# Gate and up of two feed-forward layers by Strassen's 2x2 block product

## Chip, cores and metric

The kernel runs on one core of one Trainium2 chip. The metric is the device time of one execution in microseconds (us), given as the median of several runs. The times of single instructions come from one execution that the hardware profiler recorded.

## What is computed

One inference step of a two-layer decoder trunk on 520 tokens (512 of a prompt, 8 of a sample group), with 1024 features, all in fp32. Each layer runs a SwiGLU feed-forward layer (`ffn1`), a mixer (layer 0: a chunked gated MLP; layer 1: the S5 state-space mixer), cross-attention into 256 memory tokens, and a second feed-forward layer (`ffn2`). The change touches the feed-forward layers of layer 1:

```python
def _swiglu(h, wg, wu, wd):
    return (jax.nn.silu(h @ wg) * (h @ wu)) @ wd
...
        x = x + 0.5 * _swiglu(_rmsnorm(x, norm_ffn1[i]), ffn1_wg[i], ffn1_wu[i], ffn1_wd[i])
```

`wg` and `wu` are 1024 x 2816, `wd` is 2816 x 1024. The keys and values of the memory tokens (`_mem_kv`) are also outputs.

## The kernel before

The activations stay in SBUF in transposed form, `X`: eight tiles of 128 features by 520 tokens. Products are made exact enough by splitting each fp32 operand into a high part, rounded to the fast fp32r type, and a low part that holds the rest; a product is then three matmuls (high x high, high x low, low x high). A matmul has 128 x 128 weights and 260 moving columns, half of the tokens, since an accumulation tile (`ps`, four of them in a ring) has two halves.

A weight block of 256 columns is loaded by SyncE's DMA queue into a raw buffer (`wr`, a ring of three). ScalarE copies the high part (`wh`), and VectorE, or GpSimd for every fourth call, subtracts to get the low part (`wl`); both are rings of four tiles (`wsplit`). So a weight can be split as soon as the one four before it has been used.

A feed-forward layer goes through eleven blocks of gate and up columns (`gu`). A block has 2 x 2 products of eight 128-row steps. VectorE scales each result by the norm's factor on its way out of PSUM, ScalarE applies SiLU, VectorE multiplies, and the hidden tile is split in two parts for the next product. After some blocks `down` multiplies the hidden tiles so far and accumulates into `X`; the gate-up blocks run one ahead of the groups in `FFN_GROUPS`.

Work of other stages is filled in between: each block and each `down` ends with `fill()`, which runs one step of a generator. `s5_prep` (25 steps, line 901) builds the tables of the S5 mixer, mostly with small VectorE and GpSimd instructions; it is spread over `ffn2` of layer 0 and `ffn1` of layer 1, followed by the first two steps of `mem_kv` for layer 1 (line 415: norm of the memory tokens, then their transposes). The other eight steps of `mem_kv`, the chunks of keys and values, are filled into the S5 mixer (line 1146). That mixer first needs the norm (sum of squares, `rs_tok`, `rs_diag`, `rs_row`), then runs a loop over eight feature tiles, each with a scan on VectorE.

The kernel is written as a program order; a scheduler sets the order in which the instructions of one engine stand, and each engine then runs its own list in order. Tiles that are asked for wait for the release of the tile that had the buffer. Temporaries (`t`, also `e1` to `e3` after the change) come from one ring.

## Time and profile before

| | |
|---|---|
| median of three runs | 2488.09 us (2486.79 to 2488.33) |
| the profiled execution | 2482.45 us, span 2480.7 us |
| TensorE busy | 2412.5 us (97%), 20159 matmuls |
| VectorE / ScalarE / GpSimd busy | 1343.5 (54%) / 799.7 (32%) / 558.2 us (23%) |

The profile's busy times of TensorE include the pipeline of overlapping matmuls: the 284 ns of one matmul is its own length, and the distance from one to the next is read by counting matmuls in a stretch. PE is TensorE, DVE is VectorE, ACT is ScalarE, POOL is GpSimd and SP is SyncE; PEld are the weight loads. A line such as L74 is a line of the kernel before; helpers collect many operations on one line, so the names of the tiles matter more.

### The profile page before, as it was taken

The numbers are of one execution on the slowest core, as the hardware profiler recorded it, in microseconds if no ns is written. First come the engines' busy times: TensorE is split into PE (matmuls) and PEld (weight loads), VectorE is DVE, ScalarE is ACT, GpSimd is POOL, SyncE is SP. The second block draws the span as 40 slices with busy tenths as digits, with TensorE's granted clock in tenths as the row PEclk, the third lists the DMA queues.
The fourth block names the chain that finished last, engine by engine and source line by source line (L and its number), as shares of the span: only waits on it lengthen the run. The fifth ranks groups of instructions, "written<-read, shape, count | busy, mean of one in ns | idle before, by whom it ended". The sixth has DMA issues, their size and how long they took to land.

```text
span 2480.7 us, 46682 instructions
## 1 busy us (share of the span) xinstructions
PE 2412.5 (97%) x20159; PEld 2341.0 (94%) x20159; DVE 1343.5 (54%) x2304; ACT 799.7 (32%) x1219; POOL 558.2 (23%) x532
## 2 busy tenths in 40 slices
PE   8999999999999999999999999999879999999998
PEld 7999999999999799999999999998669969999998
DVE  6534344648556557455556644546974655434344
ACT  4323222432224242232343423324322334222223
POOL 2111011102111012262522515203552101101111
PEclk9999999999999999999999999999989999999999
DMA  5243432421225623324233333325723562232321
GB/s 172 90 132 120 136 103 86 120 86 59 89 93 190 230 94 91 103 94 142 98 115 103 128 107 112 132 82 179 257 93 107 170 238 86 85 104 81 99 77 52
DMA packets 235147, 293.33 MB, mean 118 GB/s; under 512 B 6910, under 2 KB 203254, under 8 KB 234942
## 3 DMA queue, kind: packets, MB, share of 16 engines
q1 hardware_dynamic: 221831, 254.87, 31.9%
q10 hardware_dynamic: 12567, 34.38, 4.0%
q8 instruction: 159, 2.61, 0.4%
q0 software_dynamic: 544, 1.10, 0.3%
q14 instruction: 46, 0.38, 0.0%
HBM read 264.77 MB, written 25.56 MB: 117 GB/s over the span
## 4 chain that ended last, share of the span: by engine, by line
PE 87%; DVE 7%; issue 2%; ACT 1%; POOL 1%; DMA 1%; DVEq 0%; ACTq 0%; SPq 0%; POOLq 0%
PE ps L74 86%; PE ps L77 1%; DVE ld L1216 1%; DVE v L795 1%; DVE xs L280 1%; DVE wl L113 1%; DVE sq L224 1%; DVE t L555 0%; DVE hid L151 0%; POOL ld L1212 0%; ACT e L575 0%; DVE bi L1115 0%; DVE t L358 0%; POOL ld L1226 0%; DMA wr<-in_x_wv 0%
## 5 line engine op out<-in xcount | busy, mean ns | idle before, releaser
L74 PE MATMUL ps<-xs,wh 128*128 128x260 f32 x7168 | 1165.6, 284 | 3.4 <-ACT xs L279 2.4
L74 PEld LDWEIGHTS ps<-xs,wh 128*128 128x128 f32 x7168 | 990.9, 189 | 7.2 <-ACT xs L279 2.9
L110 ACT ACTIVATE wh<-wr 128x1024 fp32r<-128x1024 f32 (+2 forms) x408 | 386.5, 950 | 1079.2 <-PE ps L74 984.5
L74 PE MATMUL ps<-xs,wl 128*128 128x260 f32 x3584 | 726.2, 283 | 0.0
L113 POOL TENSOR_TENSOR wl<-wr,wh 128x1024 fp32r<-128x1024 f32 (+2 forms) x107 | 241.8, 2260 | 1507.9 <-ACT wh L110 1492.8
L74 PEld LDWEIGHTS ps<-xs,wl 128*128 128x128 f32 x3584 | 555.6, 189 | 0.0
L74 PE MATMUL ps<-hid,wh 128*128 128x260 f32 (+2 forms) x2816 | 456.7, 283 | 2.8 <-ACT hid L150 1.8
L74 PEld LDWEIGHTS ps<-hid,wh 128*128 128x128 f32 x2816 | 388.8, 188 | 4.8 <-ACT hid L150 2.2
L113 DVE TENSOR_TENSOR wl<-wr,wh 128x1024 fp32r<-128x1024 f32 (+2 forms) x301 | 341.7, 1136 | 86.2 <-ACT wh L110 85.2
L74 PE MATMUL ps<-hid,wl 128*128 128x260 f32 (+2 forms) x1408 | 288.2, 283 | 0.0
L74 PEld LDWEIGHTS ps<-hid,wl 128*128 128x128 f32 x1408 | 218.6, 188 | 0.0
L358 DVE TENSOR_TENSOR t<-ps,rs 128x520 f32<-128x520 f32 x88 | 61.4, 698 | 256.0 <-PE ps L74 256.0
L372 DVE SCALAR_TENSOR_TENSOR X<-ps,X 128x520 f32<-128x520 f32 x120 | 83.8, 698 | 210.3 <-PE ps L74 209.9
L356 DVE TENSOR_TENSOR t<-ps,rs 128x520 f32<-128x520 f32 x88 | 61.4, 698 | 183.7 <-PE ps L74 152.9
L151 DVE TENSOR_TENSOR hid<-t,hid 128x520 fp32r<-128x520 f32 x88 | 95.6, 1086 | 34.3 <-ACT hid L150 34.3
L150 ACT ACTIVATE hid<-t 128x520 fp32r<-128x520 f32 x88 | 56.3, 639 | 127.9 <-DVE t L359 127.8
L74 PE MATMUL ps<-o,wh 128*128 128x260 f32 x512 | 92.4, 290 | 1.2 <-DVE o L151 0.7
L74 PE MATMUL ps<-z,wh 128*128 128x260 f32 x512 | 84.2, 285 | 1.1 <-DVE z L151 0.5
L74 PE MATMUL ps<-um,wh 128*128 128x260 f32 x512 | 82.7, 284 | 0.0
L359 DVE TENSOR_TENSOR t<-t,t 128x520 f32<-128x520 f32 x88 | 78.9, 897 | 6.8 <-ACT wh L121 0.5
L74 PEld LDWEIGHTS ps<-o,wh 128*128 128x128 f32 x512 | 74.6, 188 | 7.4 <-issue 2.9
L74 PE MATMUL ps<-t,ld 128*32 128x136 f32 (+1 forms) x896 | 49.1, 326 | 26.2 <-POOL t L1221 9.2
(321 smaller groups left out, 2409.9 us busy)
## 6 DMA issues: line engine op xcount, KB each, us to landing
wr<-in_ffn_wg SPq DMA_DIRECT2D x43, 1024.0 KB
wr<-in_ffn_wu SPq DMA_DIRECT2D x43, 1024.0 KB, 5.5
wr<-in_ffn_wd SPq DMA_DIRECT2D x48, 768.0 KB, 4.2
wr<-in_a_w_in SPq DMA_DIRECT2D x16, 1024.0 KB, 6.1
kc<-in_cache_mem_k SPq DMA_DIRECT2D x32, 512.0 KB, 7.4
vc<-in_cache_mem_v SPq DMA_DIRECT2D x32, 512.0 KB, 6.1
wr<-in_x_wk SPq DMA_DIRECT2D x8, 1024.0 KB, 5.0
wr<-in_x_wv SPq DMA_DIRECT2D x8, 1024.0 KB, 5.7
```

The source lines that it names most:

```text
L74: self.nc.tensor.matmul(out, lhsT=lhsT, rhs=rhs, start=start, stop=stop)
L77: self.nc.tensor.transpose(out, in_, self.ident[base : base + k, base : base + k])
L110: nc.scalar.activation(hi, r, AF.Copy)
L113: eng.tensor_sub(lo, r, hi.bitcast(F32))
L150: nc.scalar.activation(sl[:, 0, n0:n1], src, AF.Copy)
L151: nc.vector.tensor_sub(sl[:, 1, n0:n1], src, sl.bitcast(F32)[:, 0, n0:n1])
L224: (nc.gpsimd if k == 7 and early or k < 4 and not early else nc.vector).tensor_add(sums[-1], sums[-1], t)
L280: self.nc.vector.scalar_tensor_tensor(s[:, 1, n0:n1], x, g, s.bitcast(F32)[:, 0, n0:n1], op0=ALU.mult, op1=ALU.subtract)
L356: nc.vector.tensor_mul(self.v2(t), pg[:, :, :HN], rs)
L358: nc.vector.tensor_mul(self.v2(w), pu[:, :, :HN], rs)
L359: nc.vector.tensor_mul(w, w, t)
L372: nc.vector.scalar_tensor_tensor(xv, p[:, :, :HN], 0.5, xv, op0=ALU.mult, op1=ALU.add)
```

## The change

In both feed-forward layers of layer 1 the first two gate-up blocks stay as they were (`PLAIN`); the other nine go through `gu7`. The 1024 input features and 256 columns of a block are cut in two, and the tokens are cut in two. With A the weights and B the inputs, seven products of half size replace eight. `seven_x` makes the combinations of the inputs once per layer, `seven` those of the weights in each block: S1 and S2 on GpSimd, S3 and the second S2 on VectorE. Results are collected in three accumulation tiles and three temporaries. All seven low parts of a block are VectorE's. The groups for `down` have four hidden tiles (two in the last). The raw buffers become four, the temporaries nine instead of twelve. `s5_prep` runs two steps per filling in `ffn2` of layer 0 alone, and all of `mem_kv` for layer 1 is filled into the S5 mixer, where two fillings follow each other behind `rs_diag` and the loop fills in all eight rounds.

```diff
+WR = 4
 FFN_GROUPS = ((0, 6), (6, 12), (12, 18), (18, 22))
-BUFS = {"t": 12, "rs": 2, "rt": 4, "st": 10, "sti": 4, "mv": 4, "sc": 2, "cj": 2, "s5": 12, "s5i": 1,
+SEVEN_GROUPS = ((0, 4), (4, 8), (8, 12), (12, 16), (16, 20), (20, 22))
+PLAIN = 2
+BUFS = {"t": 9, "rs": 2, "rt": 4, "st": 10, "sti": 4, "mv": 4, "sc": 2, "cj": 2, "s5": 12, "s5i": 1,
...
+    def seven_x(self, key, xs):
+        nc = self.nc
+        V = nc.vector
+        xb = [[self.slot([128, 4, HN], F32, "xb") for _ in range(2)] for _ in range(2)]
+        for k in range(KT):
+            for h in range(2):
+                nc.scalar.activation(xb[k // 4][h][:, k % 4], self.X[:, k, h * HN : (h + 1) * HN], AF.Copy,
+                                     scale=self.gcol(key, k))
+        (b11, b12), (b21, b22) = xb
+        V.tensor_sub(b11, b12, b11)
+        V.tensor_sub(b12, b22, b12)
+        V.tensor_sub(b22, b22, b11)
+        V.tensor_sub(b21, b21, b22)
+        T = []
+        for b in (b11, b22, b12):
+            hi, lo = (self.slot([128, 4, HN], F32R, "xt") for _ in range(2))
+            nc.scalar.activation(hi, b, AF.Copy)
+            V.tensor_sub(lo, b, hi.bitcast(F32))
+            T.append([(hi[:, k], lo[:, k]) for k in range(4)])
...
+        def last():
+            for k in range(4):
+                self.split(xs[k], b21[:, k], HN, NT)
+
+        return {"B11": B[0], "B21": B[2], "B22": B[3], "T1": T[0], "T2": T[1], "T3": T[2], "T4": B[1]}, last
+
+    def seven(self, r1, r2, ops, ps):
+        A11, A21, A12, A22 = r1[..., :128], r1[..., 128:], r2[..., :128], r2[..., 128:]
+        n, nk = sh[1:3]
...
+        def product(p, w, b, first):
+            hi, lo = w
+            for x in range(n):
+                for k in range(nk):
+                    bh, bl = ops[b][k]
+                    for i, (m, r) in enumerate(((hi, bh), (hi, bl), (lo, bh))):
+                        self.mm(p[:, x, :HN], m[:, x, k], r, first and k == 0 and i == 0, k == nk - 1 and i == 2,
+                                skip_group_check=not first)
+
+        S1, S2, S3 = (self.wp.tile(sh, F32, name=self.nm("S"), tag="S", bufs=3) for _ in range(3))
+        w11 = parts(A11)
+        G.tensor_add(S1, A21, A22)
+        G.tensor_sub(S2, S1, A11)
+        a, b, c = (ps() for _ in range(3))
+        va, vb, vc = (p[:, :, :HN] for p in (a, b, c))
+        e1, e2, e3 = (self.tmp([128, 2, HN]) for _ in range(3))
+        product(a, w11, "B11", True)
+        nc.scalar.copy(e1, va)
+        product(b, parts(S2), "T2", True)
+        V.tensor_add(e2, vb, e1)
+        product(a, parts(A12), "B21", False)
+        yield "11", va
+        V.tensor_sub(S3, A11, A21)
+        V.tensor_sub(S2, A12, S2)
+        product(b, parts(S3), "T3", False)
+        V.tensor_add(e3, vb, e1)
+        product(c, parts(S1), "T1", True)
+        V.tensor_add(e3, vc, e3)
+        yield "22", e3
+        product(b, parts(A22), "T4", False)
+        V.tensor_add(e1, vb, e1)
+        yield "21", e1
+        product(c, parts(S2), "B22", False)
+        V.tensor_add(e2, vc, e2)
+        yield "12", e2
...
+        def gu7(j):
+            if late:
+                late.pop()()
+            cs = slice(j * 256, (j + 1) * 256)
...
+            tw = [self.tmp() for _ in range(2)]
+            for name, v in self.seven(*r, ops, self.ps):
+                i, h = int(name[0]) - 1, int(name[1]) - 1
+                d = self.tmp([128, 2, HN]) if name == "11" else v
+                nc.vector.tensor_mul(d, v, rs[:, h : h + 1].to_broadcast([128, 2, HN]))
+                nc.scalar.activation(d[:, 0], d[:, 0], AF.Silu)
+                nc.vector.tensor_mul(tw[i][:, h * HN : (h + 1) * HN], d[:, 1], d[:, 0])
+                if name in ("21", "12"):
+                    hid[2 * j + i] = self.slot(name="hid")
+                    self.split(hid[2 * j + i], tw[i])
+            fill()
...
-                gu(done)
+                (gu7 if seven and done >= PLAIN else gu)(done)
                 done += 1
+                if seven and done == 1:
+                    ops, more = self.seven_x(key, xs)
+                    late.append(more)
...
-            nc.gpsimd.dma_start(bn[:, c], ins["b_b_" + n][0].rearrange("(q g) p c -> (g p) q c", g=2))
+            for q in range(0, NPAIR, 8):
+                nc.gpsimd.dma_start(bn[:, c, q : q + 8],
+                                    ins["b_b_" + n][0, 2 * q : 2 * q + 16].rearrange("(q g) p c -> (g p) q c", g=2))
...
         dg = self.rs_diag(sq)
         fill()
+        fill()
         rs = self.rs_row(dg)
...
-            if i < KT - 2:
-                fill()
+            fill()
...
-        self.ffn(0, False, steps(prep))
+        self.ffn(0, False, steps(prep, 2))
+        drain(prep)
         self.tap("ffn2_0")
-        pre = chain(prep, islice(gen := self.mem_kv(1, kv1), 2))
-        self.ffn(1, True, steps(pre))
-        drain(pre)
+        self.ffn(1, True, seven=True)
         self.tap("ffn1_1")
         self.pool_every = 2
+        gen = self.mem_kv(1, kv1)
         self.s5(steps(gen))
...
-        self.ffn(1, False, finish=self.final)
+        self.ffn(1, False, finish=self.final, seven=True)
```

VectorE, in `ffn1` of layer 1, where two gate-up blocks meet. Before (L356 and L358 scale gate and up, L113 is a low part, L151 the split of a hidden tile):

```order
L356 TENSOR_TENSOR t_15784<-ps_15686,rs_14258 128x520
L113 TENSOR_TENSOR wl_15949<-wr_15946,wh_15948 128x1024
L358 TENSOR_TENSOR t_15785<-ps_15687,rs_14258 128x520
L359 TENSOR_TENSOR t_15785<-t_15785,t_15784 128x520
L113 TENSOR_TENSOR wl_15953<-wr_15946,wh_15952 128x1024
L151 TENSOR_TENSOR hid_15790<-t_15785,hid_15790 128x520
```

And after, in the first block of a pair (L342 is a low part, L365, L371 and L373 the adds e2, e3, e3, L474 a scaling, L476 the gated product, L368 the S3 and L369 the second S2 of the next block):

```order
L342 TENSOR_TENSOR wl_15825<-S_15692,wh_15824 128x1024
L365 TENSOR_TENSOR t_15705<-ps_15702,t_15704 128x520
L342 TENSOR_TENSOR wl_15857<-wr_15687,wh_15856 128x1024
L474 TENSOR_TENSOR t_15789<-ps_15701,rs_14798 128x520
L342 TENSOR_TENSOR wl_15892<-S_15693,wh_15891 128x1024
L476 TENSOR_TENSOR t_15690<-t_15789 128x260
L368 TENSOR_TENSOR S_15936<-wr_15926 128x1024
L371 TENSOR_TENSOR t_15706<-ps_15702,t_15704 128x520
L342 TENSOR_TENSOR wl_15938<-wr_15926,wh_15937 128x1024
L373 TENSOR_TENSOR t_15706<-ps_15703,t_15706 128x520
L474 TENSOR_TENSOR t_15706<-t_15706,rs_14798 128x520
L342 TENSOR_TENSOR wl_15975<-S_15935,wh_15974 128x1024
```

Between the adds that read the accumulation tiles there now stand low parts and S3 of the next block.

GpSimd, in the second feed-forward layer of layer 0, around a step that builds `M`. Before (L1063 to L1069 build M, L113 is every fourth low part):

```order
L1066 TENSOR_TENSOR t_11287<-Bb_10679,pw 128x128
L1061 TENSOR_TENSOR t_11291<-CT_10411,pw 128x128
L1062 TENSOR_TENSOR t_11292<-CT_10411,pw 128x128
L1065 TENSOR_TENSOR t_11296<-CT_10411,pw 128x128
L1066 TENSOR_TENSOR t_11297<-CT_10411,pw 128x128
L1061 TENSOR_TENSOR t_11302<-Bb_10679,pw 128x128
L1062 TENSOR_TENSOR t_11303<-Bb_10679,pw 128x128
L113 TENSOR_TENSOR wl_11374<-wr_11367,wh_11373 128x1024
L1063 TENSOR_TENSOR M_11279<-t_11281,t_11282 128x8x16
```

And after, at the end of the third such step (L1189 and L1191 build M, L1207 to L1227 are the step behind it, L116 is the low part):

```order
L1189 TENSOR_TENSOR M_12242<-t_12313,t_12314 128x8x16
L1207 MEMSET Es_12664 128x1024
L1191 TENSOR_SCALAR M_12242<-M_12242 128x8x16
L1207 MEMSET t_12665 128x256
L1219 TENSOR_SCALAR t_12682<-t_9941,w4h 128x128 x4
L1221 TENSOR_TENSOR t_12682<-t_12682,t_12683 128x512
L1227 TENSOR_TENSOR t_12682<-t_12682,t_12694 128x512
L116 TENSOR_TENSOR wl_12584<-wr_12577,wh_12583 128x768
```

The low part of the last weight of that `down` stage now stands behind both steps.

TensorE, from the last `down` of `ffn1` of layer 1 into the S5 mixer. Before (`ms` are the normed memory tokens, `sq` the squares of the norm):

```order
L74 MATMUL ps_18575<-hid_18350,wl_18546 128x260 x2
L74 MATMUL ps_18626<-wh_18629,ms_17737 128x512 x4
L74 MATMUL ps_18626<-wl_18630,ms_17737 128x512 x2
L74 MATMUL ps_18626<-wh_18629,ms_17737 128x512 x4
L74 MATMUL ps_18626<-wl_18630,ms_17737 128x512 x2
L74 MATMUL ps_18626<-wh_18645,ms_17738 128x512 x4
L74 MATMUL ps_18626<-wl_18646,ms_17738 128x512 x2
L74 MATMUL ps_18626<-wh_18645,ms_17738 128x512 x4
L74 MATMUL ps_18626<-wl_18646,ms_17738 128x512 x2
L74 MATMUL ps_18661<-ones,sq_18601 128x1 x5
```

And after (`mem` are the memory tokens before their transposes):

```order
L77 MATMUL ps_18750<-hid_18326,wl_18733 128x260 x2
L77 MATMUL ps_18820<-ones,sq_18764 128x1 x5
L80 MATMUL ps_18853<-ident,mem_18787 128x128
L80 MATMUL ps_18870<-ident,mem_18787 128x128
L80 MATMUL ps_18853<-ident,mem_18788 128x128
```

A first chunk of keys stood between the last `down` product and the sums of squares; now the sums come at once, and the transposes behind them.

## Rows read from the trace of the kernel before

**Rows 1.** The page: the span, the first line of the busy times, and the shares of the chain that ended last, by engine.

```profile
span 2480.7 us, 46682 instructions
PE 2412.5 (97%) x20159; PEld 2341.0 (94%) x20159; DVE 1343.5 (54%) x2304; ACT 799.7 (32%) x1219; POOL 558.2 (23%) x532
PE 87%; DVE 7%; issue 2%; ACT 1%; POOL 1%; DMA 1%; DVEq 0%; ACTq 0%; SPq 0%; POOLq 0%
```

**Rows 2.** Busy time in stretches of the span: first 62 us inside the last feed-forward layer, then the second feed-forward layer of layer 0, the first of layer 1, and the start and the loop of the S5 mixer. Columns: the stretch, its length, then busy us and (x instructions) of PE, PEld, DVE, ACT and POOL, the granted clock, the DMA share and GB/s.

```profile
2170.00:2232.00 62.00, 62.00 (x520) 62.00 (x520) 24.29 (x27) 15.54 (x18) 6.08 (x3) 1.00 0.34 107
934.00:1312.00 378.00, 373.49 (x3136) 371.03 (x3135) 217.91 (x360) 124.14 (x189) 135.99 (x164) 1.00 0.35 109
1312.00:1705.00 393.00, 388.88 (x3269) 385.88 (x3269) 207.73 (x324) 127.51 (x198) 124.49 (x154) 1.00 0.33 109
1705.40:1738.70 33.30, 33.30 (x217) 27.64 (x216) 26.46 (x44) 16.11 (x19) 15.72 (x22) 1.00 0.77 261
1738.70:1846.00 107.30, 80.01 (x1156) 70.48 (x1154) 101.35 (x155) 30.07 (x67) 56.54 (x62) 0.90 0.58 193
```

**Rows 3.** The timeline of VectorE and GpSimd in places. Columns: start, length in us, engine, line, operation, out<-in. Two pairs that follow each other without a wait, then a GpSimd subtraction and a VectorE add beside it, then a low part beside a run of GpSimd instructions.

```profile
1723.51 1.23 DVE L124 TENSOR_TENSOR wl<-wr,wh 128x1024 fp32r<-128x1024 f32 x1
1724.65 1.20 DVE L1164 SCALAR_TENSOR_TENSOR t<-X,gains,rs 128x512 f32<-128x512 f32 x1
1735.04 0.68 DVE L1208 TENSOR_TENSOR ld<-ps,ld 128x512 f32<-128x512 f32 x1
1735.64 0.68 DVE L1209 TENSOR_TENSOR ld<-ps,ld 128x512 f32<-128x512 f32 x1
1700.84 2.40 POOL L124 TENSOR_TENSOR wl<-wr,wh 128x1024 fp32r<-128x1024 f32 x1 [3.60 <-ACT wh L121]
1701.32 2.48 DVE L224 TENSOR_TENSOR sq<-sq,sq 128x520 f32<-128x520 f32 x1 [0.74 <-ACT sq L220]
1077.10 3.48 DVE L113 TENSOR_TENSOR wl<-wr,wh 128x1024 fp32r<-128x1024 f32 x1
```

**Rows 4.** Groups of instructions by line and shape over the whole span: count | busy us, mean ns of one | idle time before them and what ended it.

```profile
L151 DVE TENSOR_TENSOR hid<-t,hid 128x520 fp32r<-128x520 f32 x88 | 95.6, 1086 | 34.3 <-ACT hid L150 34.3
L372 DVE SCALAR_TENSOR_TENSOR X<-ps,X 128x520 f32<-128x520 f32 x120 | 83.8, 698 | 210.3 <-PE ps L74 209.9
L110 ACT ACTIVATE wh<-wr 128x1024 fp32r<-128x1024 f32 x256 | 270.7, 1060 | 754.4 <-PE ps L74 669.1 <-issue 60.0 <-DVE t L1136 21.6
L220 ACT ACTIVATE sq<-X 128x520 f32<-128x520 f32 x62 | 37.4, 626 | 2.3 <-DVE X L372 2.3
L113 POOL TENSOR_TENSOR wl<-wr,wh 128x768 fp32r<-128x768 f32 x24 | 44.1, 1839 | 325.4 <-ACT wh L110 325.4
```

**Rows 5.** The step that builds M in the second feed-forward layer of layer 0, from the timeline of GpSimd (its first instruction, and two of the step behind it) and of VectorE (a scaling that waited for a temporary); then a line of TensorE's waits over the span: us in total, times, longest.

```profile
1068.24 0.92 POOL L1063 TENSOR_TENSOR M<-t,t 128x128 f32<-128x128 f32 x1
1076.48 0.70 DVE L356 TENSOR_TENSOR t<-ps,rs 128x520 f32<-128x520 f32 x1 [7.65 <-POOL M L1063]
1087.78 2.35 POOL L1097 TENSOR_SCALAR t<-t,w4h 128x128 f32<-128x128 f32 x4
1096.94 1.29 POOL L1105 TENSOR_TENSOR t<-t,t 128x512 f32<-128x512 f32 x1 [0.60 <-DVE t L1104]
PE ps L77 <- DVE t L1122: 5.2, 6, 1.2
```

**Rows 6.** The start of the S5 mixer in the timeline: on TensorE the first matmuls of a chunk of keys behind the last down product, the sums of squares, and the diagonal product; on VectorE one of the small instructions of the norm.

```profile
1705.41 1.09 PE L74 MATMUL ps<-wh,ms 128*128 128x512 f32 x4
1710.96 1.17 PE L74 MATMUL ps<-ones,sq 128*128 128x1 f32 x10
1717.57 1.04 PE L74 MATMUL ps<-dg,ones 128*128 128x260 f32 x4
1715.17 0.17 DVE L244 SCALAR_TENSOR_TENSOR t<-t,t 128x5 f32<-128x5 f32 x1
```

**Rows 7.** The chain that ended last, in the loop of the S5 mixer: the scans of rounds 0, 4 and 5. Columns: start, length, engine, out, line.

```profile
1738.70 3.58 DVE ld L1216 x8
1800.81 3.67 DVE ld L1216 x8
1814.13 3.69 DVE ld L1216 x8
```

**Rows 8.** Three stretches of 4 us around gaps of TensorE (columns as in rows 2; the granted clock is third from the right), and from the timeline the matmuls that ended the first two gaps, with the gap in brackets.

```profile
598.00:602.00 4.00, 1.62 (x7) 1.63 (x8) 4.00 (x4) 1.16 (x2) 3.92 (x2) 0.77 0.01 4
600.38 2.07 PE L74 MATMUL ps<-wt,v 128*128 128x128 f32 x8 [2.60 <-DVE t L781]
1312.00:1316.00 4.00, 4.00 (x26) 4.00 (x26) 2.90 (x13) 0.00 (x0) 0.00 (x0) 0.69 0.54 185
1311.47 1.25 PE L74 MATMUL ps<-ones,sq 128*128 128x1 f32 x10 [0.76 <-DVE sq L225]
1336.00:1340.00 4.00, 3.30 (x28) 3.09 (x28) 3.84 (x11) 0.00 (x0) 3.37 (x8) 1.00 0.91 294
```

**Rows 9.** The last down stage: a step of TensorE from the chain that ended last, and two adds of the last norm on GpSimd from the timeline.

```profile
2457.93 2.85 PE ps L74 x24
2463.10 1.55 POOL L1345 TENSOR_TENSOR sq<-sq,sq 128x256 f32<-128x256 f32 x2 [4.16 <-ACT sq L1341]
```

More of the change, by code (lines that the diff above doesn't have):

```diff
@@ L2 @@
 from contextlib import ExitStack, contextmanager
-from itertools import chain, islice
+from itertools import chain
 import concourse.bass as bass
@@ L71, in const, with mm @@
         return self.cp.tile(list(shape), dt, name=name, tag=name)
-    def mm(self, out, lhsT, rhs, start, stop):
-        self.nc.tensor.matmul(out, lhsT=lhsT, rhs=rhs, start=start, stop=stop)
+    def mm(self, out, lhsT, rhs, start, stop, **kw):
+        self.nc.tensor.matmul(out, lhsT=lhsT, rhs=rhs, start=start, stop=stop, **kw)
     def tr(self, out, in_, k=128, base=0):
@@ L97, in wraw @@
     def wraw(self, nk, cols):
-        return self.wp.tile([128, nk, cols], F32, name=self.nm("wr"), tag="wr", bufs=3)
+        return self.wp.tile([128, nk, cols], F32, name=self.nm("wr"), tag="wr", bufs=WR)
     def wget(self, raw, src, c0, c1):
@@ L287, in norm @@
         return xs, self.squares()
-    def ffn(self, l, pre, fill=lambda: None, start=False, finish=None):
+    def seven_x(self, key, xs):
[17 more added lines that the diff above has]
+            T.append([(hi[:, k], lo[:, k]) for k in range(4)])
+        B = [[(xs[4 * i + k][:, 0, h * HN : (h + 1) * HN], xs[4 * i + k][:, 1, h * HN : (h + 1) * HN])
+              for k in range(4)] for i, h in ((0, 0), (0, 1), (1, 0), (1, 1))]
+        def last():
+            for k in range(4):
+                self.split(xs[k], b21[:, k], HN, NT)
+        return {"B11": B[0], "B21": B[2], "B22": B[3], "T1": T[0], "T2": T[1], "T3": T[2], "T4": B[1]}, last
@@ new lines, in seven, with parts @@
+    def seven(self, r1, r2, ops, ps):
+        nc = self.nc
+        V, G = nc.vector, nc.gpsimd
+        sh = list(r1.shape[:3]) + [128]
+        A11, A21, A12, A22 = r1[..., :128], r1[..., 128:], r2[..., :128], r2[..., 128:]
+        n, nk = sh[1:3]
+        def parts(src):
+            hi = self.wp.tile(sh, F32R, name=self.nm("wh"), tag="wh", bufs=WB)
+            lo = self.wp.tile(sh, F32R, name=self.nm("wl"), tag="wl", bufs=WB)
+            nc.scalar.activation(hi, src, AF.Copy)
+            V.tensor_sub(lo, src, hi.bitcast(F32))
+            return hi, lo
+        def product(p, w, b, first):
[32 more added lines that the diff above has]
+        yield "12", e2
@@ L291, in ffn @@
+    def ffn(self, l, pre, fill=lambda: None, start=False, finish=None, seven=False):
         nc, ins = self.nc, self.ins
@@ L363, in gu @@
             fill()
+        ops, late = None, []
+        def gu7(j):
+            if late:
+                late.pop()()
+            cs = slice(j * 256, (j + 1) * 256)
+            r = []
+            for i in range(2):
+                r.append(self.wp.tile([128, 2, 4, 256], F32, name=self.nm("wr"), tag="wr", bufs=WR))
+                for x, w in enumerate((wg, wu)):
+                    nc.sync.dma_start(r[i][:, x], w[i * 512 : (i + 1) * 512, cs].rearrange("(k p) m -> p k m", p=128))
+            tw = [self.tmp() for _ in range(2)]
[9 more added lines that the diff above has]
+            fill()
         def down(a, b):
@@ L404, in ffn @@
         done = 0
-        for g0, g1 in FFN_GROUPS:
+        for g0, g1 in SEVEN_GROUPS if seven else FFN_GROUPS:
             while done < min(DFF // 256, g1 // 2 + 1):
-                gu(done)
+                (gu7 if seven and done >= PLAIN else gu)(done)
                 done += 1
+                if seven and done == 1:
+                    ops, more = self.seven_x(key, xs)
+                    late.append(more)
             if g1 == DFF // 128 and finish:
@@ L1403, in run, with steps, go @@
     def run(self):
-        def steps(gen):
-            return lambda: next(gen, None)
+        def steps(gen, n=1):
+            def go():
+                for _ in range(n):
+                    next(gen, None)
+            return go
         def drain(gen):
```

2 lines of the change are left out of this document (1 added, 1 removed).

## The prediction

> **What bounds the kernel now.** I read the page's first part first: TensorE is busy 97% of a span of 2480.7 us, VectorE 54%, ScalarE 32%, GpSimd 23%, and the chain that ended last is 87% TensorE [rows 1]. Busy can flatter TensorE, so next I cut the span into stages. Inside the last feed-forward layer, 62 us hold 520 matmuls of 260 columns without a gap: 62 / 520 = 0.1192 us each. VectorE works 24 of those 62 us [rows 2]. There every removed matmul is worth its 0.1192 us, as long as the other engines can still follow. The two layers around the preparation of the S5 mixer (934 to 1705 us) lose some 9 us of TensorE in 771 us. Only the loop of the S5 mixer is different: from 1738.7 to 1846 us TensorE is busy 80 of 107 us and VectorE 101 [rows 2]. So the gain is made where TensorE is the limit, and I have to price what the change adds to VectorE, GpSimd, and that loop.
>
> **Removed.** A plain block of 256 gate and up columns is 2 x 2 x 8 x 3 x 2 = 192 matmuls. A block of seven products is 7 x 2 x 4 x 3 = 168. Nine of eleven blocks change in each of two layers: 18 x 24 = 432 matmuls, and the order of instructions holds 432 fewer of them. 432 x 0.1192 = **-51.5 us**. A product of 24 matmuls lasts 2.86 us, a block 20.0 us instead of 22.9. The down products keep their number.
>
> **Added to VectorE in a block.** Instructions that follow one another start 1.14 us apart for 1024 elements and 0.61 apart for about 520 [rows 3]. A block of seven has nine of 1024 (seven low parts, S3, the second S2), eleven of 520 (five combining adds, four scalings, two splits) and four of 260, which I estimate at 0.34, a little over half of 0.61: 10.3 + 6.7 + 1.4 = 18.4 us. A plain block has three low parts (the fourth is GpSimd's) and eight of 520: 8.3 us. So in a block VectorE goes from 36% to 92% of TensorE's time. Two blocks and one down stage of four hidden tiles make a round: 40.1 + 22.9 us of TensorE against some 47 of VectorE, so it keeps up on average. What counts is where it is late. Three times in a block TensorE must wait until VectorE has read a sum out of PSUM before it adds to it (the adds e2, e3 and again e3), with one product, 2.86 us, as cover.
>
> I walk the first block of a pair, time 0 at its first product. Product 3 ends at 8.6. Then VectorE has the scaling of result 11 (0.7), the low part of the second S2, which can only start after ScalarE's 1.06 us copy [rows 4] at 9.9 and ends at 11.1, a multiplication to 11.5, S3 of the next block to 12.6, then the add e3 to 13.2. TensorE needs it at 14.3: it fits by 1.1. GpSimd computes S1 and S2 of the next block, 2.40 us each when undisturbed [rows 3]; its S2 becomes ready at 11.2, when the buffer of the old one is free. What happens then is in the trace: an add with both operands in SBUF that should take 0.7 took 2.48 us beside a GpSimd subtraction and ended just after it, and a low part took 3.48 instead of 1.23 during a run of GpSimd instructions, while a VectorE instruction that reads PSUM kept its 0.70 in that same run [rows 3, 5]. Over all calls the hidden split averages 1086 ns, the accumulation from PSUM 698 [rows 4]. So if GpSimd's S2 gets in ahead of S3, e3 ends at 15.6 and TensorE loses 1.3 us; if S3 gets in first, nothing is lost, because e3 reads PSUM. I take 0.9 for each of 4 pairs in 2 layers: **+7 us**, bounds 0 (GpSimd always in VectorE's waits) and 3.2 x 18 = 58 (each block's 4.8 us of GpSimd put end to end with 18.4 of VectorE, 23.2 against 20.0). I stay near the lower end since S1 falls into a wait for ScalarE and the second block's partner is computed under the down stage.
>
> The Trainium skill speaks against the change here ("SBUF — State Buffer", section "Who interferes with whom"): an instruction with two SBUF inputs and a GpSimd one that reads SBUF exclude each other for their whole length. The trace agrees on both sides. Taken to its end the rule is the second rival below.
>
> The first Strassen block of a layer stands apart: the split of T4 overwrites half of the input that the second plain block still reads, and in VectorE's order two of those splits stand ahead of the low part for product 2. VectorE therefore starts from zero at the block's start: 2 x 0.34 of split after ScalarE's, low part at 2.6, two splits, low part at 4.5, second S2 5.7, the plain block's last three at 0.61 each between two low parts and the hidden split, e2 at about 10.5 against 8.6: 1.9 us late, in each layer: **+4** (0 to 6).
>
> **The S5 preparation, two steps a filling.** All 25 steps now lie in the second feed-forward layer of layer 0. The matmul work is the same; the six waits on line L1122, 5.2 us together, only move [rows 5]. New is that a step that builds M (GpSimd from 1068.24 to about 1087.5, 19.3 us [rows 5]) is followed without a pause by the step behind it, and that the pool of temporaries shrinks from 12 to 9, so the next scaling waits longer for GpSimd than the 7.65 us it did [rows 5]. It had 22.9 us of cover (four accumulation tiles). Queued behind the pair on GpSimd is every fourth low part. I looked where that is due early: the last weight of the second down stage stands behind an M step and the next step; M starts some 3.6 us into the stage and ends at 23; the next step, which took from 1087.5 to 1098.2 with a low part of 2.40 between, so 8.3 us [rows 5], brings 31, the low part's own 1.84 [rows 4] 33. It is due after seven of the stage's eight weights, 7 x 4.29 = 30 us (36 matmuls each): 3 us late. Three other pairs fit within 1 us. **+5** (0; 24, if each of four M pairs costs 6).
>
> **The S5 mixer.** Before, three fillings cover the wait for the norm: TensorE goes from 1705.41 without a gap, has the norm's column sums at 1710.96, the diagonal product at 1717.57 [rows 6]. Now the first two fillings are the memory tokens' norm and transposes, so TensorE has nothing between the last down product and the sums: 0.7 + 0.64 + 0.7 + 0.7 (accumulation, square, two adds [rows 4]) and hand-overs, 3.2 us. The memory norm's four squares (about 0.8 each on ScalarE with the read of the sum, an estimate from the 626 ns of its other squares [rows 4]) and a second chain of 12 small VectorE instructions of 0.17, some 0.2 apart [rows 6], then hold up the norm's own chain: diagonal after about 12.5 instead of 11.2, its product behind half a chunk at some 18, the first scan at about 30 after the last down product instead of 1738.70 - 1705.4 = 33.3. So the loop starts 3 us earlier, but 2.5 of the eight chunks of memory keys and values have moved into it. In the loop a chunk costs less than its 5.5 us of TensorE: the four scan intervals with chunks add up to 62.1 us, one with the layout and no chunk is 13.3 [rows 7], so (62.1 - 4 x 13.3) / 4 = 2.2 each. 2.5 x 2.2 - 3 = +2.5; TensorE comes out of the idle stretch at half clock for some matmuls: **+3** together (bounds -5, chunks free; +16, each at its 5.5 and no earlier start). For the clock: in the 4 us around a gap of 2.60 us the granted clock is 0.77, after one of 0.76 with nothing but ten matmuls of one column behind it 0.69, and around a gap of 0.70 among full matmuls it stays 1.00 [rows 8]. So I price short waits between full products at their own length.
>
> **The tail.** The last stage has two hidden tiles instead of four: 1.4 us of TensorE per step where 2.85 stood [rows 9]. Each step carries about 1.55 us of GpSimd adds [rows 9]; the first half's sums come 2 us after TensorE could use them: **+2** (0 to 4). The extra 16 accumulations per layer (0.61) and the inputs T1 to T4 (some 10 us of VectorE) lie under the down stages and the two plain blocks, 45.8 us; without that cover they would cost 20 a layer. Weight loads: the same bytes, and the fourth raw buffer lets both halves of a block arrive before the block in front ends.
>
> **Sum.** -51.5 + 7 + 4 + 5 + 3 + 2 = -30.5. The profiled execution took 2482.45 us (span 2480.7), so 2452; the median of the runs shown, 2488.09, is 5.6 above it, so **2458 us**.
>
> **Rivals.** (1) Everything is covered: no late add, preparation and S5 neutral, only the tail: -49.5, 2438.6. For it: VectorE's 18.4 us fit into 20.0. Against: three hand-overs per block with 1.1 to 2 us of slack. (2) VectorE and GpSimd put end to end become the bound of the blocks: 23.2 us a block, more than the plain 22.9. -51.5 + 58 + 14 gives 2508: slower. It decides once an add that TensorE waits for comes more than 2.86 us after its product in most blocks, that is, with TensorE under 90% in them. Against it: half of GpSimd's adds fall under down stages. (3) The preparation packed into one layer costs 24 instead of 5: 2477. For it: GpSimd is busy 136 us of 378 in that layer and 124 in the next [rows 2], and most of the second comes on top of the first. (4) The change does not do what it says: a matmul of the products would have to take 0.136 us to eat the gain (51.5 / 3024 more); every weight is already loaded anew for each matmul (20159 loads for 20159 matmuls [rows 1]), so the other order costs nothing that I see.
>
> **Chances.** Forecast 0.55 (its own range 2445 to 2472), rival (1) 0.20, (2) 0.10, (3) 0.13, (4) 0.02. The range of 2438 to 2484 takes in (1) and (3) and leaves out (2) and the worst of (3). A change of 0.2% (5 us, 2483 to 2493) is about the least that can be told from none here. Faster: 0.55 + 0.20 + 0.08 of (3) = 0.83; the same 0.07; slower 0.10.
>
> **What would show it.** Right: TensorE 97 to 100% busy inside the block pairs of the last layer, small waits on line L371 or L365's adds only; VectorE above 70% there; a gap of some 10 us at the start of the S5 mixer, a loop a few us longer; small waits in the second feed-forward layer. Wrong: waits of 2 us and more on the combining adds in each block (rival 2), on GpSimd's low parts or on temporaries in the second layer (rival 3), or matmuls of the products more than 0.12 us apart (rival 4).

## The result and the profile after

The changed kernel took 2515.69 us (median of four runs, 2511.70 to 2519.97), the kernel before 2488.21 beside it: 1.0109 times as long, with a 95% interval of 1.0090 to 1.0129. The forecast was 2458. The profiled execution took 2519.97 us, its span is 2518.1, so the rows below account for 37.4 us and the medians for 27.5.

The page of the kernel after, with the lines of [rows 1]:

```profile
span 2518.1 us, 46658 instructions
PE 2389.8 (95%) x19727; PEld 2312.3 (92%) x19727; DVE 1566.1 (62%) x2616; ACT 897.8 (36%) x1405; POOL 602.1 (24%) x564
PE 82%; DVE 8%; POOL 5%; ACT 2%; issue 2%; DMA 1%; ACTq 0%; POOLq 0%; DVEq 0%
```

432 matmuls fewer, as planned, but TensorE's busy time fell by 22.7 us alone: the matmuls that are left took some 29 us longer. The granted clock is 0.972 on the mean of the whole execution; before, it is 0.990. TensorE's idle time rose by 60. The stretches of [rows 2], and three of the layer with the preparation, one around its second long gap, and the start of the S5 mixer (columns as in [rows 2]):

```profile
2170.00:2232.00 62.00, 62.00 (x520) 62.00 (x519) 50.03 (x61) 30.80 (x51) 8.96 (x5) 1.00 0.33 103
992.00:1054.00 62.00, 53.13 (x419) 51.21 (x418) 32.23 (x54) 21.92 (x43) 42.69 (x66) 0.89 0.36 123
1054.00:1116.00 62.00, 61.26 (x521) 60.68 (x519) 25.10 (x35) 14.46 (x20) 29.25 (x55) 1.00 0.28 89
1116.00:1178.00 62.00, 50.30 (x400) 48.74 (x401) 37.21 (x70) 19.33 (x38) 34.97 (x63) 0.89 0.34 120
1122.00:1144.00 22.00, 17.41 (x118) 16.39 (x119) 17.64 (x34) 10.87 (x24) 10.16 (x11) 0.73 0.44 157
1740.00:1764.00 24.00, 13.91 (x65) 12.16 (x64) 17.57 (x49) 10.56 (x21) 5.31 (x6) 0.72 0.35 125
```

The first line is the design at work: in the blocks of seven TensorE has no gap at all, 520 matmuls in 62 us as before, with VectorE at 50 us instead of 24. Lines two to five are the layer with the preparation, where before 378 us lost 4.5: here 62 us lose 9, 1 and 12, and behind a long gap the granted clock is 0.73 on the mean of 22 us, that is, part of them at the lower of its two levels (1.2 GHz instead of 2.4). TensorE is busy in 17.4 of these 22 us.

To see where the 37.4 us are, I cut both spans where the sums of squares of each norm start on TensorE (as the second line of [rows 6] shows for the S5 mixer):

| stage, from one norm's sums to the next | before | after | difference |
|---|---|---|---|
| up to the second feed-forward layer of layer 0 | 915.9 | 919.9 | +4.0 |
| that layer, with the S5 preparation | 395.6 | 466.1 | +70.5 |
| first feed-forward layer of layer 1 | 399.5 | 362.8 | -36.7 |
| S5 mixer | 231.3 | 241.7 | +10.4 |
| attention | 146.3 | 150.3 | +4.0 |
| last feed-forward layer, to the end | 392.1 | 377.3 | -14.8 |

The first and the fifth line are no finding: over the runs below these two stages vary by as much, whatever is changed elsewhere (914.8 to 921.4, and 146.3 to 150.3).

TensorE's waits in the layer with the preparation (us in total, times, longest):

```profile
PE ps L80 <- POOL Es L1207: 15.5, 2, 8.6
PE ps L80 <- DVE t L449: 13.1, 2, 6.7
PE ps L80 <- DVE t L1244: 5.0, 3, 2.5
PE ps L80 <- DVE t L1034: 4.3, 1, 4.3
```

L80 is the transpose; in these rows it turns Bs and other tiles of the preparation. So TensorE stands at the preparation's own transposes. What they wait for, from the timeline of GpSimd, ScalarE, VectorE and TensorE around the second gap:

```profile
1095.95 0.92 POOL L1185 TENSOR_TENSOR M<-t,t 128x128 f32<-128x128 f32 x1
1112.38 0.95 POOL L1207 MEMSET Bs<- 128x1024 f32 x1
1113.36 1.67 ACT L1211 COPY Bs<-M 64x256 f32<-64x256 f32 x4 [14.50 <-POOL Bs L1207]
1117.67 1.06 ACT L113 ACTIVATE wh<-wr 128x1024 fp32r<-128x1024 f32 x1 [0.25 <-ACT t L1213]
1117.76 0.43 DVE L1220 TENSOR_SCALAR t<-t 128x512 f32<-128x512 f32 x1 [17.47 <-POOL t L1219]
1121.09 0.69 DVE L449 TENSOR_TENSOR t<-ps,rs 128x520 f32<-128x520 f32 x1
1121.93 1.94 PE L80 MATMUL ps<-ident,Bs 128*128 128x128 f32 x8 [6.67 <-DVE t L449]
```

GpSimd builds M from 1095.95 on. ScalarE's next instruction is the first copy into Bs; it waits 14.50 us, until GpSimd has cleared Bs, and behind it stands the weight copy of 1117.67, a copy of the layer's own. VectorE waits 17.47 us for the scaled phases of the same step, and behind that stands the eviction of the layer's accumulation at 1121.09. TensorE runs out of both and stops for 6.67 us. In the kernel before, the first copy of such a step waited 1.41 us. Over the execution ScalarE waits for GpSimd's clearing of Bs six times in either kernel, 10.6 us in total before and 48.7 after. That copy:

```profile
1095.47 1.25 ACT L1089 COPY Bs<-M 64x256 f32<-64x256 f32 x3 [1.41 <-POOL Bs L1085]
```

The second new wait is at the start of each layer of seven. VectorE, GpSimd and TensorE behind the last attention:

```profile
2142.68 0.17 DVE L244 TENSOR_TENSOR t<-t,t 128x5 f32<-128x5 f32 x1
2145.31 2.36 DVE L244 TENSOR_TENSOR t<-t,t 128x5 f32<-128x5 f32 x1
2147.90 2.20 DVE L247 SCALAR_TENSOR_TENSOR t<-t,t 128x5 f32<-128x5 f32 x1
2144.17 3.47 POOL L357 TENSOR_TENSOR S<-wr,wr 128x1024 f32<-128x1024 f32 x1 [5.86 <-DMA wr<-in_ffn_wu]
2147.72 2.36 POOL L358 TENSOR_TENSOR S<-S,wr 128x1024 f32<-128x1024 f32 x1
2151.56 2.07 PE L77 MATMUL ps<-dg,ones 128*128 128x260 f32 x4 [3.68 <-DVE dg L265]
```

Two instructions of five columns, whose kind takes 0.17 us, took 2.36 and 2.20, each until one of GpSimd's two sums of 1024 elements was done. They are links in the norm's chain, so the diagonal comes 3.68 us late, where in the kernel before TensorE did not wait.

The start of the S5 mixer, with the lines of [rows 6], and the scans of its loop (duration min/median/max in ns, first and last start):

```profile
1748.79 2.27 PE L77 MATMUL ps<-ones,sq 128*128 128x1 f32 x10 [7.44 <-DVE t L546]
1763.38 1.04 PE L77 MATMUL ps<-dg,ones 128*128 128x260 f32 x4
L1339 DVE TENSOR_TENSOR_SCAN ld<-mag,ld x64: 391/398/2618, 1784.0 to 1888.5; 128x128 f32<-128x128 f32 x64
```

The last down product ends at 1741.35. The norm's sums wait 7.44 us, the diagonal product comes 22.0 us after the down product (12.2 before) and the first scan 42.6 after it (33.3 before). From the first of the eight scan groups to the start of the last (1885.21 in the chain of waits) it is 101.2 us; before, 99.3 [rows 7, with a last one at 1838.04].

At the tail, for [rows 9], TensorE's waits in the last 119 us:

```profile
PE ps L77 <- DVE sq L1467: 1.9, 1, 1.9
PE ps L77 <- POOL sq L1467: 0.4, 1, 0.4
```

### The profile page after: what moved, and what is told of

Same layout as the page of the kernel before. It is cut to its first block, busy times and chain, and to the rows that moved or that the text cites. A ratio compares the mean times of both kernels' runs of the same rounds, so it can differ in the third digit from the quotient of the medians.

```text
span 2518.1 us, 46658 instructions
## 1 busy us (share of the span) xinstructions
PE 2389.8 (95%) x19727; PEld 2312.3 (92%) x19727; DVE 1566.1 (62%) x2616; ACT 897.8 (36%) x1405; POOL 602.1 (24%) x564
## 4 chain that ended last, share of the span: by engine, by line
PE 82%; DVE 8%; POOL 5%; ACT 2%; issue 2%; DMA 1%; ACTq 0%; POOLq 0%; DVEq 0%
PE ps L77 81%; PE ps L80 2%; DVE ld L1339 1%; POOL wl L116 1%; DVE v L915 1%; DVE sq L227 1%; DVE wl L116 1%; DVE t L675 0%; DMA vc<-in_cache_mem_v 0%; POOL t L1219 0%; POOL M L1185 0%; DVE xs L283 0%; ACT wh L113 0%; POOL M L1189 0%; POOL ld L1335 0%
## 5 line engine op out<-in xcount | busy, mean ns | idle before, releaser
L77 PE MATMUL ps<-xs,wh 128*128 128x260 f32 x6016 | 1010.2, 286 | 5.4 <-ACT xs L282 2.4
L77 PEld LDWEIGHTS ps<-xs,wh 128*128 128x128 f32 x6016 | 859.2, 191 | 9.7 <-ACT xs L282 3.0
L113 ACT ACTIVATE wh<-wr 128x1024 fp32r<-128x1024 f32 (+3 forms) x368 | 318.7, 868 | 821.9 <-PE ps L77 733.1
L116 POOL TENSOR_TENSOR wl<-wr,wh 128x1024 fp32r<-128x1024 f32 (+3 forms) x97 | 196.8, 2029 | 1334.8 <-ACT wh L113 1332.0
L77 PE MATMUL ps<-hid,wh 128*128 128x260 f32 (+1 forms) x2816 | 459.5, 285 | 5.0 <-DVE X L489 2.2
L116 DVE TENSOR_TENSOR wl<-wr,wh 128x1024 fp32r<-128x1024 f32 (+3 forms) x271 | 280.1, 1033 | 81.1 <-ACT wh L113 80.7
L77 PE MATMUL ps<-xt,wh 128*128 128x260 f32 x864 | 156.9, 282 | 0.0
L77 PEld LDWEIGHTS ps<-xt,wh 128*128 128x128 f32 x864 | 133.3, 188 | 0.0
L77 PE MATMUL ps<-xt,wl 128*128 128x260 f32 x432 | 122.2, 283 | 0.0
L342 DVE TENSOR_TENSOR wl<-S,wh 128x1024 fp32r<-128x1024 f32 x72 | 93.0, 1291 | 21.4 <-ACT wh L341 21.4
```

The source lines that it names most:

```text
L77: self.nc.tensor.matmul(out, lhsT=lhsT, rhs=rhs, start=start, stop=stop, **kw)
L113: nc.scalar.activation(hi, r, AF.Copy)
L116: eng.tensor_sub(lo, r, hi.bitcast(F32))
L342: V.tensor_sub(lo, src, hi.bitcast(F32))
```

## The experiments

**Is it the pairs of steps, the temporaries, or the product itself?** Four kernels on one chip.

*Packed*: the kernel before, with plain blocks and 12 temporaries.

```diff
-        self.ffn(0, False, steps(prep))
-        pre = chain(prep, islice(gen := self.mem_kv(1, kv1), 2))
+        self.ffn(0, False, steps(prep, 2))
+        drain(prep)
+        pre = islice(gen := self.mem_kv(1, kv1), 2)
```

> The kernel before with one edit: in the second feed-forward layer of layer 0 every filling issues two steps of the S5 preparation, and what is left of it is issued at that layer's end. Blocks stay plain, temporaries stay 12. Theory A (a step that builds M and the step behind it in one filling: ScalarE's copies of Bs and VectorE's scaling of pt then wait for all of M on GpSimd, and the layer's own weight copies and evictions stand behind them): TensorE loses what the kernel after loses there, about 54 us, so 2530 to 2550 us. Theory B (the smaller ring of temporaries makes the loss): at most 10 us more than before, 2488 to 2498. My forecast's term of 5 would give 2493.

Measured: 2542.5 us, 1.0213 times before (1.0195 to 1.0231). TensorE's waits in the layer:

```profile
PE ps L77 <- POOL Es L1085: 14.5, 2, 7.5
PE ps L77 <- DVE t L356: 10.7, 2, 5.6
PE ps L77 <- DVE t L1122: 5.0, 3, 2.2
```

They are after's waits, each line within 2.4 us, without any product of seven. The layer takes 463.9 us (after: 466.1), the next one 383.7, which is 15.8 less than before: that much of the next layer's time was preparation and has only moved. So the packing costs 466.1 - (395.6 + 15.8) = 54.7 us.

*Temps9*: the kernel before.

```diff
-BUFS = {"t": 12, "rs": 2, "rt": 4, "st": 10, "sti": 4, "mv": 4, "sc": 2, "cj": 2, "s5": 12, "s5i": 1,
+BUFS = {"t": 9, "rs": 2, "rt": 4, "st": 10, "sti": 4, "mv": 4, "sc": 2, "cj": 2, "s5": 12, "s5i": 1,
```

> The kernel before with 9 temporaries instead of 12 and nothing else. Theory A (pairs of steps): within 8 us of before, since evictions wait 7.65 us for a temporary once. Theory B (temporaries): 2520 us or more, because every eviction in the two layers with the preparation has to wait for GpSimd to be done with its temporaries.

Measured: 2487.53 us, 0.9997 (0.9987 to 1.0006). The smaller ring costs nothing where steps come singly; theory B is out as a cause of its own.

*Unpaired*: the kernel after; each filling takes its number of steps from a list.

```diff
-        self.ffn(0, False, steps(prep, 2))
+        self.ffn(0, False, steps(prep, (2, 2, 2, 1, 2, 2, 1, 2, 2, 1, 2, 2, 1, 2)))
```

> The kernel after with another grouping of the same 25 steps over the same 14 fillings: 2, 2, 2, 1, 2, 2, 1, 2, 2, 1, 2, 2, 1, 2, so that a step that builds M always comes last in its filling and the next step that copies out of it comes one filling later. Theory A: the long waits of ScalarE and VectorE for GpSimd go, TensorE's waits in this layer fall from 47 us to under 15, and the time falls by 40 to 55 us to 2460 to 2476. Theory B (temporaries) and theory C (the layer simply holds too much work for GpSimd, 200 of 460 us): the same steps, the same ring, so 2500 us or more.

Measured: 2481.39 us, 0.9974 (0.9964 to 0.9984), 34 less than after. A copy into Bs on ScalarE, and the start of the next layer's norm on TensorE:

```profile
1052.70 0.41 ACT L1211 COPY Bs<-M 64x256 f32<-64x256 f32 x1 [3.40 <-POOL Bs L1207]
1350.15 2.26 PE L77 MATMUL ps<-ones,sq 128*128 128x1 f32 x10 [6.63 <-DVE sq L228]
```

The copy's wait falls from 14.50 to 3.40, all six together from 48.7 to 24.8, and the layer from 466.1 to 433.5 with the same steps: theories B and C are out as the main cause. It fell short of my 40 to 55: TensorE's waits in the layer fall from 46 us to 19, not under 15, and 22 us over 395.6 + 15.8 are left. The last step, issued at the layer's end, now stands in VectorE's queue ahead of the next norm: 7.3 us of TensorE's waits are on the scaled input, and then 6.63 on the sums. The last run below moves that step forward and has neither wait.

*Seven_last*: the kernel after, with the fillings of the kernel before.

```diff
+        pre = chain(prep, islice(gen := self.mem_kv(1, kv1), 2))
-        self.ffn(1, True, seven=True)
+        self.ffn(1, True, steps(pre))
...
         self.ffn(1, False, finish=self.final, seven=True)
```

> The kernel after with the products of seven in the last feed-forward layer alone; preparation, memory steps and S5 mixer are filled as before (9 temporaries, four raw buffers). It prices the product itself: 216 matmuls fewer are 25.7 us. My forecast's terms (3.5 for the pairs, 2 for the first block, 1 to 2 for the tail) give 2488 - 19 = 2469. The trace of after (block pairs without a gap, but the norm's diagonal 3.7 us late and half clock behind it) gives a stage that is 14 to 15 us shorter: 2473. If VectorE and GpSimd disturbed each other in every block, 2495 or more.

Measured: 2470.89 us, 0.9929 (0.9913 to 0.9946), so 16.6 less than before with 216 matmuls fewer. Beside a short wait in the tail there is one new wait in the layer, the one on the diagonal:

```profile
PE ps L77 <- DVE dg L265: 3.7, 1, 3.7
```

**What delays the norm's diagonal?** Two kernels, on one chip with mem_early and combo. In both, VectorE's S3 stands behind the diagonal; they differ in GpSimd's two sums, which stand behind it in the first alone.

*Hold_s1*: the kernel after; hold is the last instruction of the norm's diagonal, given for the first block of seven alone.

```diff
-        G.tensor_add(S1, A21, A22)
+        s1 = G.tensor_add(S1, A21, A22)
+        if hold:
+            self.tc.add_manual_dep(s1.ins, hold.ins.name, mybir.DependencyInfo(
+                mybir.DependencyClass.Sync, mybir.DependencyReason.DATA), reason="hold")
```

> The kernel after; in each layer of seven GpSimd's sum S1 for the first block of seven (and so S2 behind it) is held until the norm's diagonal is written. In the order S3 then also stands behind the diagonal. Theory D (GpSimd's two sums of 1024 elements lie beside the norm's chain and keep VectorE's small two-operand instructions waiting, 2.36 and 2.20 us instead of 0.17): the chain runs through, TensorE's wait of 3.7 us on the diagonal and the half clock behind it go, 5 to 7 us in each of two layers: 2501 to 2506. Theory E (what delays the chain is the row of VectorE instructions put in between, a low part and S3): the same gain as in the other run, where S3 alone is held.

Measured: 2500.45 us, 1.0053 (1.0037 to 1.0070). VectorE's chain, its diagonal, and GpSimd's S1:

```profile
2128.33 0.16 DVE L247 SCALAR_TENSOR_TENSOR t<-t,t 128x5 f32<-128x5 f32 x1
2129.72 0.88 DVE L265 TENSOR_SCALAR dg<-ident,t 128x128 f32<-128x128 f32 x4
2130.82 3.29 POOL L357 TENSOR_TENSOR S<-wr,wr 128x1024 f32<-128x1024 f32 x1 [8.28 <-DVE dg L266]
```

*Hold_s3*: the kernel after.

```diff
-        V.tensor_sub(S3, A11, A21)
+        s3 = V.tensor_sub(S3, A11, A21)
+        if hold:
+            self.tc.add_manual_dep(s3.ins, hold.ins.name, mybir.DependencyInfo(
+                mybir.DependencyClass.Sync, mybir.DependencyReason.DATA), reason="hold")
```

> The kernel after; only VectorE's S3 of the first block of seven is held behind the norm's diagonal, GpSimd's S1 and S2 are as before. VectorE's order around the chain is the one of the run that holds S1. Theory D (GpSimd): the chain still has its two instructions of over 2 us, TensorE still waits 2.5 to 3.7 us, at most 3 us gained: 2512 to 2516. Theory E (VectorE's own row): as much as the other run, 2501 to 2506.

Measured: 2508.49 us, 1.0087 (1.0070 to 1.0104). The chain and GpSimd's sums:

```profile
2136.46 2.37 DVE L247 SCALAR_TENSOR_TENSOR t<-t,t 128x5 f32<-128x5 f32 x1
2139.06 2.23 DVE L245 SCALAR_TENSOR_TENSOR t<-t,t 128x5 f32<-128x5 f32 x1
2136.01 2.79 POOL L357 TENSOR_TENSOR S<-wr,wr 128x1024 f32<-128x1024 f32 x1 [5.34 <-DMA wr<-in_ffn_wu]
2138.88 2.38 POOL L358 TENSOR_TENSOR S<-S,wr 128x1024 f32<-128x1024 f32 x1
```

With the same order on VectorE, two links still last 2.37 and 2.23 us while GpSimd's sums run, and TensorE waits 2.7 us in each layer instead of 3.7; with S1 held the links last 0.16 and 0.17, the wait is gone, and TensorE is busy through the whole start. So most of it is GpSimd's doing (theory D), 1.0 of 3.7 us is VectorE's S3. By stages, holding S1, with S3 behind it, gives 5.5 us in the first layer of seven (362.8 to 357.3) and 6.6 in the last (377.3 to 370.7): 12.1. Holding S3 gives 1.0 and 3.8 by stages, 1.5 of it in the tail, which varies by as much in other runs.

**Are the memory steps the mixer's loss?**

*Mem_early*: the kernel after; the mixer fills as the kernel before does.

```diff
-        self.ffn(1, True, seven=True)
+        gen = self.mem_kv(1, kv1)
+        self.ffn(1, True, steps(gen, (0,) * 13 + (1, 1)), seven=True)
```

> The kernel after; the first two steps of the second layer's memory keys and values (its norm and its transposes) are issued in the last two fillings of the first feed-forward layer of layer 1, and the S5 mixer fills as the kernel before does. Theory: the S5 mixer's start (TensorE's waits of 7.4, 2.6 and 5.6 us and its half clock) and its loop go back to what they were, so 13 to 19 us less, 2497 to 2503. Rival: blocks of seven have no room for the two steps (VectorE at 80%), and the gain is under 6 us.

Measured: 2516.35 us, 1.0117 (1.0102 to 1.0133): nothing gained. The sums and the scans:

```profile
1753.55 2.26 PE L77 MATMUL ps<-ones,sq 128*128 128x1 f32 x10 [3.91 <-DVE sq L228]
L1338 DVE TENSOR_TENSOR_SCAN ld<-mag,ld x64: 390/398/2556, 1784.2 to 1886.9; 128x128 f32<-128x128 f32 x64
```

My theory fell. With the fillings of before, and the last down product done at 1743.9, the sums still come 9.6 us after it (5.5 before) and the first scan 40.3 (33.3 before). The feed-forward stage became 7.2 us longer, the mixer's 6.6 shorter: the loss moved. In after, the diagonal product comes 14.6 us behind the sums (6.6 before). VectorE has written the diagonal by 1755.8, but TensorE has the transposes, which wait 2.65 us, and half a chunk of keys ahead of the product. Here it comes 9.5 us behind the sums, but the sums themselves are 4.1 us later than before.

The sums are late where the layer in front is one of seven. In seven_last it has plain blocks and the mixer has the fillings of this run, and there the sums come 5.5 us and the first scan 33.4 us after the last down product, as before. VectorE at the end of the layer of seven, in after:

```profile
1741.27 2.20 DVE L127 TENSOR_TENSOR wl<-wr,wh 128x1024 fp32r<-128x1024 f32 x1
1744.00 3.84 DVE L227 TENSOR_TENSOR sq<-sq,sq 128x520 f32<-128x520 f32 x3
```

A low part of the mixer's weights takes 2.20 us where the same takes 1.23 [rows 3], beside one that GpSimd makes from 1739.66 to 1742.39. The last accumulation into X stands behind it, at 1743.39, and the adds of the squares behind that. The last down stage of a layer of seven has two hidden tiles instead of four, so these instructions have half the cover. That fits; I did not run the layer with another last group, so which part of it makes the sums late is argued, not shown.

**Is it my own step, the low parts queued on GpSimd?**

*Low_dve*: the kernel after.

```diff
+        self.pool_every = 10**6
         self.ffn(0, False, steps(prep, 2))
         drain(prep)
+        self.pool_every = 4
```

> The kernel after; in the second feed-forward layer of layer 0 no low part of a weight goes to GpSimd any more (VectorE makes all of them), everything else as in after. My forecast's step said that a pair of steps costs what the low parts queued behind it on GpSimd are late: if that were the loss, some 40 to 50 us go, 2466 to 2476. Theory A (ScalarE's and VectorE's own queues stand behind instructions that wait for M): the waits on the scaling and the memsets stay, 2505 to 2520.

Measured: 2493.24 us, 1.0028 (1.0016 to 1.0041), between the two expectations. The waits:

```profile
PE ps L80 <- DVE t L449: 10.7, 2, 5.5
PE ps L80 <- POOL Es L1207: 9.5, 2, 4.8
```

The layer falls from 466.1 to 447.5, 18.6 of the 54.7 us. The long waits stay, shorter by 1.2 to 3.8 us each; that fits the low part of 2.80 us that stands ahead of M on GpSimd in after, from 1093.19 on. So the low parts make the queue longer, but the larger part, as unpaired shows, is ScalarE and VectorE standing at M.

**All repairs together, and the better choice of them.**

*Combo*: the kernel after with the edits of hold_s1, hold_s3 and mem_early, and

```diff
+        next(prep)
+        self.ffn(0, False, steps(prep, (1, 2, 2, 1, 2, 2, 1, 2, 2, 1, 2, 2, 1, 2)))
+        self.ffn(1, True, steps(chain(prep, gen), (1,) + (0,) * 12 + (1, 1)), seven=True)
```

> The kernel after with the three repairs together: preparation steps regrouped so that no step follows an M step in one filling (the first issued ahead of the layer, the last in the next layer's first block), S1 and S3 of the first block of seven held behind the norm's diagonal, and the memory steps early. If the three losses are separate, 2515.7 less 34 (regrouping as measured), 8 to 14 (its rest: the norm that collided with the last step, and the wait for the parameters), 10 to 14 and 13 to 19: 2435 to 2450. If they hide each other, 2455 to 2475. Before is 2488.

Measured: 2471.70 us, 0.9938 (0.9923 to 0.9952), as if the repairs hid each other. The preparation's layer is at 418.5 us, but the next at 380.7: its first block now carries the last step, and TensorE then waits 4.52 us in the first block of seven for a low part that VectorE owes it. That layer and the mixer take 613.3 us together; in the next run, without the moved step and the early memory steps, 597.6. Which of the two moves costs how much, these runs do not show.

*Best*: the kernel after with the edits of hold_s1 and hold_s3, and

```diff
+        next(prep)
+        self.ffn(0, False, steps(prep, (3, 2, 1, 2, 2, 1, 2, 2, 1, 2, 2, 1, 2, 1)))
```

> The kernel after with two of the repairs: the preparation's first step ahead of the layer and the other 24 over its 14 fillings as 3, 2, 1, 2, 2, 1, 2, 2, 1, 2, 2, 1, 2, 1 (no step behind an M step in one filling, the last bi step well before the next layer's norm), and S1 and S3 of the first block of seven held behind the norm's diagonal. The S5 mixer fills as in after. From the stages of the runs so far: 917 up to the layer, 420 in it, 597 for the next layer and the mixer, 147 for the attention, 371 for the rest, so a span of 2452 and about 2455 us (2448 to 2465). If the earlier steps collide with the layer's own norm or wait for their DMAs, 2465 to 2475, no better than seven products in the last layer alone (2471).

Measured: 2460.06 us, 0.9891 (0.9873 to 0.9910): faster than both kernels. Its page, and the longest waits in the layer of the preparation, which takes 422.7 us:

```profile
span 2460.1 us, 46657 instructions
PE 2371.5 (96%) x19727; PEld 2298.7 (93%) x19727; DVE 1565.7 (64%) x2616; ACT 894.8 (36%) x1405; POOL 606.6 (25%) x564
PE ps L80 <- DVE t L1247: 4.9, 6, 1.2
PE ps L80 <- DVE hb L1172: 4.6, 1, 4.6
```

The first wait is a cost that the kernel before has too [rows 5]; the second is the price of three steps in the first filling: unpaired and combo, with two and one there, do not have it.

## Why the prediction was wrong

**Removed, -51.5: right.** The blocks of seven run 520 matmuls in 62 us, so every removed matmul was worth its 0.1192. With both layers' starts repaired, the last layer and the tail take 21.4 us less than before of the 25.7.

**Adds in the block pairs, +7: nothing.** No combining add is waited for anywhere. VectorE takes 50 of 62 us, near my 47 a round, and rival (2), with TensorE under 90%, is false. The rule that GpSimd and VectorE exclude each other held, in another place.

**First block of seven, +4: measured +12 (S1 and S3 held), another mechanism.** I looked for the loss at e2 and at the split of T4; the block runs without a gap. I had not asked what the block's sums do while they are computed ahead of it. GpSimd starts S1 as soon as the block's weights have landed (its wait above is for their DMA; that the fourth raw buffer brings them so early is argued, no run took it back), and that is beside the norm's chain of small VectorE instructions, on which TensorE waits. I had even read such a pair in [rows 3], an add of 2.48 us beside a GpSimd subtraction, and used it only inside the blocks. The Trainium skill says of this ("SBUF — State Buffer", section "Who interferes with whom") that such instructions exclude each other for their whole length; the rows agree with it here: 2.36 and 2.20 us, and 0.17 when GpSimd's sum is moved away. The norm of the S5 mixer in the kernel before would have pointed there: of its chain of 0.17 us instructions [rows 6], one took 2.17 beside a low part on GpSimd, though it reads a single tile.

```profile
1711.89 2.40 POOL L124 TENSOR_TENSOR wl<-wr,wh 128x1024 fp32r<-128x1024 f32 x1 [2.92 <-ACT wh L121]
1712.37 2.17 DVE L237 TENSOR_SCALAR t<-t 128x5 int32<-128x5 int32 x1
```

**Preparation, +5 (0 to 24): measured +54.7. This is the step that failed.** I wrote that "queued behind the pair on GpSimd is every fourth low part" and priced that queue. The instructions of the second step stand on ScalarE and VectorE too, wait there for M, and in those queues stand the layer's weight copies and evictions. M takes about 19 us [rows 5], and the step behind it was issued one filling later before, by when M was done. The runs show 18.6 us that go with the low parts, 32.6 that go with the regrouping of the same steps (466.1 to 433.5), and 43.4 (to 422.7) in the last run, where the first step is also issued ahead of the layer. The low parts' share and the regrouping's overlap. My upper bound of 24 came from the same queue, so it bounded nothing. Rival (3), the right place at 24, was under half of it. Half clock behind the gaps is part of the 54.7: I had priced gaps at their own length, from rows with short ones [rows 8].

**S5 mixer, +3 (-5 to +16): measured about +11**, 9.3 at the start and 1.9 in the loop. The loop is cheaper than the 5.5 I gave the chunks (2.5 at 2.2 each), and the last run, with the same fillings, has its scans within 102.5 us from first to last where after has 104.5 and mem_early, with the fillings of before, 102.7: no run shows a price of the moved chunks. The start, which I had 3 us earlier, is 9 later. I had the sums some 3 us after the last down product, and they came after 7.4. I had the first scan some 12 us behind the diagonal product; it came after 20.6, and before it was 21.1 [rows 6, 7]: that term had no row behind it. Why the start is late is settled only in part: the sums are late behind a layer of seven, the transposes and keys stand ahead of the diagonal product, and issuing the memory steps early moved the loss and did not remove it.

**Tail, +2: right** (1.9 + 0.4).

-51.5 + 0 + 12.1 + 54.7 + 11.2 + 2.3 = 28.8; with the 8 us of the two stages that vary by themselves, 36.8 of the 37.4 between the profiled executions. The median's 27.5 is near the sum without them.

## What to carry to other kernels

When prepared work is filled into another loop, a step that waits for a long job on one engine must not be issued before that job has had time to end: in-order queues hand its wait to everything behind it, on every engine that the step uses. Price a filling by its instructions on each engine, and count the time between the one that makes and the one that takes. When an operand's buffer lets sums run ahead, ask what small chain on a shared path they will land beside.
